# Values of the short set first, from channel-major inputs that are not normalised, in a hybrid mLSTM and dilated-attention encoder layer

## The chip, the cores and the metric

The kernel runs on one core of one Trainium2 chip. The metric is the device time of one execution in microseconds (us). Times of several executions are given as a median with the lowest and the highest.

## The reference

One encoder layer is applied with the same weights to two token sets, the long set A (1024 tokens) and the short set B (512 tokens), each token with 1024 channels, all in float32:

```
h      = x * rsqrt(mean(x*x) + eps) * pre_w            # RMSNorm over channels
cols   = h @ w_in                                      # 1024 -> 12304 columns
m_qk, m_v, m_o, m_z, m_i, m_f, a_qkv, a_z, gate = split(cols)
y_m    = mlstm(conv_silu(m_qk), m_v, m_i, m_f) * sigmoid(m_o) * silu(m_z)
y_a    = dilated_attention(a_qkv) * silu(a_z)
merged = sig(g_A) * (y_m @ w_pm) + sig(g_B) * (y_a @ w_pa)
out    = x + RMSNorm(merged @ w_out) * post_w
```

The change touches only the first two lines, and of the columns above all the "values": `m_v` (1024 columns), the attention's v (1536) and the 16 columns of the mLSTM gates, 2576 together. The row norm is one number per token. It therefore commutes with the projection: `(x * r * pre_w) @ w = r * ((x * pre_w) @ w)`.

## The kernel before, in words

**Three matmuls for one.** To keep float32 accuracy at TensorE's fast rate, each operand is split into a high part (a rounded copy, made by ScalarE) and a low part (the difference, made by VectorE), and `mm3` (L190 to L195) issues high x high, high x low and low x high into one PSUM bank. Weights are split on the fly, for the fill in `split_w` (L244).

**The long set's projection** is a 2 x 2 block product, tokens in two halves of 512 and channels in two halves of 512, done with seven products in place of eight. The seven combined inputs are `B11`, `T2`, `B21`, `T3`, `T1`, `T4`, `B22`, each four tiles of 128 channels by 512 tokens, split and kept in SBUF as `H`. The combined weights are made by `sums`. The value columns are done in four groups (`value_group`, g = 0 to 3), each group two blocks of `VW` = 322 columns. One product of a group is 48 matmuls with H as the stationary operand and 322 columns moving. The other columns are done by `unit_pair`, with 512 tokens moving.

**Group 0** differs from the other groups, because it also makes `H`. The tokens arrive row-major (tile `xt`, 128 tokens x 1024 channels). `root` (L253) squares a row tile on ScalarE with a running sum and computes the reciprocal root on GpSimd. `combos` returns four helpers: `lead` makes B11 by multiplying four row tiles by diagonal matrices of the root on TensorE, `norm` normalises row tiles, `sub` forms differences on VectorE, and `put` transposes a combined input into PSUM by 128 x 128 matmuls on TensorE, from where ScalarE and VectorE take the high and low parts. The generators `with_m1`, `with_m2`, `with_m7`, `with_m6` place these between the matmuls of group 0's products, in the order M1, M2, M7, M6, M5, M4, M3. A row of `pre_w` is spread over all partitions by four 512-wide matmuls (L1882) first.

**The short set's projection** is not blocked. It is done in units of 128 columns (`unit`, 24 matmuls of 512 tokens in eight steps) and, for the values, ten units of 256 columns (`value_unit`, the first with the 16 gate columns, `VG` = 272; per unit four token tiles of 24 matmuls, 16 steps of six matmuls). The units are not a stage of their own. They are a list in `Fill`, and the later stages (mLSTM of A, attention of A, mLSTM of B) call `fill(share)` between their own matmuls, so that TensorE always has work. `STEPS` says how many steps each stage takes from the list and `SHORT` is their total: 310 + 232 + 194 = 736. The list begins with eight attention units, then the ten value units. The short set's `H` (`hT`) is made by `short_input` behind the last unit of A: 32 transposes of row tiles (`xs`) that were loaded and normalised during the last eight pairs of units.

**Order of the work.** TensorE runs in the order in which the program is written (`manual_schedule`). In the first part of the program the other engines and the DMA queue of SyncE (SP) are ordered by the compiler by priority and readiness; from the fill on SP is written by hand too. `tc.issue_after(x)` keeps instructions of an engine behind x, and `high_priority` pulls weight splits forward. All PSUM products of the first part share eight banks (`d`).

The lines that the steps name: L249/L250 weight splits of the fill; L256 to L258 root; L273, L279, L280 `turn_in` (transposes of the short set's input and their high and low parts); L315 a 512-wide matmul of the bias tables; L347, L349 `lead`; L377, L379, L387 `put`; L426/L427 weight splits of the value groups; L1022 to L1044 `front` and L1078 to L1106 `core` of the long mLSTM (rm, scl, qw, ql, kl, cf, cl); L1463 to L1500 attention.

Of the kernel before, what the change touches and what calls it, by code (L numbers as in the profile page):

```python
# [43 lines left out]
VG = 256 + 16  # L44
RING = 4 * VG
# [131 lines left out]
class Net:  # L177
# [83 lines left out]
    def norm(self, xt, r, junk, pw=None):  # L261

        r = self.root(xt, r, junk)
        if pw is None:
            return self.nc.vector.tensor_scalar(xt, xt, r, None, op0=OP.mult)
        return self.nc.vector.scalar_tensor_tensor(xt, xt, r, pw, op0=OP.mult, op1=OP.mult)

    def turn_in(self, parts, ps, out, k, w=None):

        nc = self.nc  # L270
        p = ps.tile([P, BLK], F32, name="d")
        for t, x in enumerate(parts):
            nc.tensor.transpose(p[:, t * P:(t + 1) * P], x[:, k * P:(k + 1) * P], self.ident)  # L273
        hi, lo = (x[:, k] for x in out)
        if w is None:
            end = nc.scalar.activation(hi, p, AF.Copy)
            nc.vector.tensor_sub(lo, p, hi.bitcast(F32))
        else:
            end = nc.scalar.activation(hi, p, AF.Copy, scale=w)  # L279
            nc.vector.scalar_tensor_tensor(lo, p, w, hi.bitcast(F32), op0=OP.mult, op1=OP.subtract)  # L280
        return end


    def constants(self, pool):
        nc, a = self.nc, self.a
        self.ident = pool.tile([P, P], F32, name="ident")
        make_identity(nc, self.ident)
        self.mhalf = pool.tile([P, 1], F32, name="mhalf")
        nc.vector.memset(self.mhalf, -0.5)
        self.prew = pool.tile([P, KT], F32, name="prew")  # L290
# [39 lines left out]
    def combos(self, ps, H, xt, r, junk, pw, minus, again, diag):  # L330

        nc = self.nc
        part = lambda i, j: [x[:, j * BLK:(j + 1) * BLK] for x in xt[i]]
        a0, b0, a1, b1 = part(0, 0), part(0, 1), part(1, 0), part(1, 1)
        plus, neg = self.ident, minus.bitcast(F32)  # L340
        terms = {B21: [(b0, plus)], B22: [(b1, plus)], T3: [(b1, plus), (a1, neg)],
                 T1: [(a0, plus)], T2: [(b1, plus)], T4: [(b0, plus), (b1, neg)]}

        def lead():
            ps_ = [ps.tile([P, BLK], F32, name="d") for _ in range(4)]
            for t in range(4):
                nc.vector.tensor_scalar(diag[t], self.ident, self.root(xt[0][t], r[t], junk), None, op0=OP.mult)  # L347
                for k in range(4):
                    nc.tensor.matmul(ps_[k][:, t * P:(t + 1) * P], a0[t][:, k * P:(k + 1) * P], diag[t], start=t == 0,  # L349
                                     stop=True, skip_group_check=True)  # L350
            for k in range(4):
                hi, lo, w = H[0][B11][:, k], H[1][B11][:, k], self.prew[:, k:k + 1]
                nc.scalar.activation(hi, ps_[k], AF.Copy, scale=w)
                self.low = nc.vector.scalar_tensor_tensor(lo, ps_[k], w, hi.bitcast(F32), op0=OP.mult, op1=OP.subtract)  # L354

        def norm(i, t):
            if i:
                return self.norm(xt[i][t], r[4 * i + t], junk, pw)
            return nc.vector.scalar_tensor_tensor(xt[i][t], xt[i][t], r[t][:, 2:3], pw, op0=OP.mult, op1=OP.mult)

        def sub(m):
            for t in range(4):
                if m == T1:
# [4 lines left out]
        def put(m, k):  # L368

            if m == T4 and k == 0:  # L370
                again()
# [1745 lines left out]
```

## Time and profile before

| what | us |
|---|---|
| median of 3 executions (lowest, highest) | 2295.2 (2293.82, 2298.0) |
| the profiled execution | 2292.12 |
| its span, first to last instruction | 2290.3 |
| start to the first main matmul | 13.49 |
| value group 0 | 76.61 |
| value groups 1 to 3 | 156.25 |
| units of the long set | 726.78 |
| mLSTM of A, with fill (985 to 1320) | 335.00 |
| attention of A, with fill (to 1648) | 328.00 |
| mLSTM of B, with fill (to 1850) | 202.00 |
| attention of B (to 2120) | 270.00 |
| rest | 170.30 |

The stretches follow one another but for 11.87 us between the units and the mLSTM of A. PE is TensorE's matmuls, PEld its weight loads, DVE VectorE, ACT ScalarE, POOL GpSimd, SP the queue that issues most transfers. In a row of instruction groups the first number is the summed time, the second the mean in ns of one instruction, and behind the bar stands the engine's idle time before them and what ended it. The tile names are the program's, without buffer numbers. A matmul's listed duration is its latency through a pipeline, so that two neighbours overlap; the distance from start to start is what a matmul costs.

### The profile page before, as it was taken

To read this page: it belongs to the slowest core of one execution; us is meant where nothing else is said; L and a number is where in the kernel's file an instruction comes from. 1 tells how busy PE (TensorE), PEld (TensorE's weight loads), DVE (VectorE), ACT (ScalarE), POOL (GpSimd) and SP (SyncE) were. 2 spreads that over 40 slices of the span, in tenths; PEclk is the share of its full clock that TensorE was granted. 3 is DMA by queue.
4 is the path that set the end of the run, shared out by engine and by line. 5 is a ranking of instruction groups with operands and counts; after the bars stand their busy time and mean duration, and the time that the engine had idled before them with its cause. 6 is when DMAs were issued, how large, how long until landed. Compare 5 with 4: busy or idle time off the path is not lost. (4 is left out here: it accounts for less than half of the span.)

```text
span 2290.3 us, 36121 instructions
## 1 busy us (share of the span) xinstructions
PE 2258.5 (99%) x12628; PEld 1975.3 (86%) x12628; DVE 1465.7 (64%) x2851; ACT 1102.2 (48%) x2255; POOL 628.6 (27%) x824
## 2 busy tenths in 40 slices
PE   9999999999999999999999999999999999999998
PEld 8999888888878888879999889988888888888887
DVE  7765577688875564466777756674487744555563
ACT  6332243444443343366667656776544444544422
POOL 2000333333332232136556510001032221421311
PEclk9999999999999999999999999999999999999999
DMA  3552455543222243285674679987687878787673
GB/s 126 161 134 71 173 204 194 195 167 113 101 102 83 83 147 110 91 315 154 219 226 138 199 195 243 249 227 214 181 254 242 254 217 241 201 256 210 216 259 113
DMA packets 251903, 416.71 MB, mean 182 GB/s; under 512 B 24993, under 2 KB 150049, under 8 KB 251722
## 3 DMA queue, kind: packets, MB, share of 16 engines
q1 hardware_dynamic: 248120, 401.82, 56.9%
q10 hardware_dynamic: 3602, 12.59, 1.4%
q8 instruction: 100, 1.64, 0.3%
q14 instruction: 81, 0.66, 0.1%
HBM read 294.34 MB, written 128.37 MB: 185 GB/s over the span
## 5 line engine op out<-in xcount | busy, mean ns | idle before, releaser
L193 PE MATMUL dense<-H,wh 128*128 128x512 f32 x672 | 277.5, 413 | 2.3 <-DVE sw L714 1.9
L195 PE MATMUL dense<-H,wl 128*128 128x512 f32 x672 | 263.8, 393 | 0.0
L194 PE MATMUL dense<-H,wh 128*128 128x512 f32 x672 | 263.0, 391 | 0.0
L195 PE MATMUL d<-Hh,phla 128*128 128x512 f32 x608 | 237.0, 390 | 2.2 <-DVE phla L610 2.2
L193 PE MATMUL d<-Hh,phla 128*128 128x512 f32 x608 | 236.6, 389 | 0.0
L194 PE MATMUL d<-Hl,phla 128*128 128x512 f32 x608 | 236.6, 389 | 0.0
L250 DVE TENSOR_TENSOR wl<-wraw,wh 128x1024 fp32r<-128x1024 f32 (+1 forms) x130 | 163.9, 1262 | 106.7 <-ACT wh L249 105.4
L1475 DVE CUSTOM_DVE_ANT_0 ls<-lg,bias 128x256 f32<-128x256 f32 (+1 forms) x288 | 93.7, 361 | 158.9 <-PE lg L1463 53.9
L249 ACT ACTIVATE wh<-wraw 128x1024 fp32r<-128x1024 f32 (+1 forms) x130 | 137.0, 1054 | 97.1 <-PE dense L194 50.0
L628 POOL TENSOR_TENSOR psum_w<-pw_raw 128x512 f32<-128x512 f32 x38 | 61.4, 1617 | 443.4 <-DVE u L596 216.0
L1479 ACT ACTIVATE ls<-ls,nm 128x256 f32<-128x256 f32 (+1 forms) x288 | 130.0, 453 | 102.9 <-DVE nm L1477 87.8
L195 PE MATMUL d<-Hh,phlb 128*128 128x512 f32 x456 | 177.4, 389 | 0.0
L193 PE MATMUL d<-Hh,phlb 128*128 128x512 f32 x456 | 177.4, 389 | 0.0
L194 PE MATMUL d<-Hl,phlb 128*128 128x512 f32 x456 | 177.4, 389 | 0.0
L195 PEld LDWEIGHTS dense<-H,wl 128*128 128x128 f32 x672 | 126.2, 188 | 28.7
L193 PEld LDWEIGHTS dense<-H,wh 128*128 128x128 f32 x672 | 126.6, 188 | 20.4 <-issue 2.3
L194 PEld LDWEIGHTS dense<-H,wh 128*128 128x128 f32 x672 | 127.0, 189 | 17.5
L194 PE MATMUL d<-vlo,Hh 128*128 128x322 f32 x448 | 139.9, 312 | 1.9 <-DVE vlo L427 1.9
L193 PE MATMUL d<-vhi,Hh 128*128 128x322 f32 x448 | 141.0, 315 | 0.3
L195 PE MATMUL d<-vhi,Hl 128*128 128x322 f32 x448 | 140.3, 313 | 0.4 <-DVE Hl L354 0.2
L195 PEld LDWEIGHTS d<-Hh,phla 128*128 128x128 f32 x608 | 114.1, 188 | 27.3 <-DVE phla L610 3.7
L194 PEld LDWEIGHTS d<-Hl,phla 128*128 128x128 f32 x608 | 114.1, 188 | 23.7
(573 smaller groups left out, 6064.2 us busy)
## 6 DMA issues: line engine op xcount, KB each, us to landing
pw_raw<-w_in SPq DMA_DIRECT2D x76, 512.0 KB
wraw<-w_in SPq DMA_DIRECT2D x76, 512.0 KB
aqk_a<-pwk SPq DMA_DIRECT2D x48, 512.0 KB
aqk_b<-sw SPq DMA_DIRECT2D x48, 256.0 KB
wraw<-w_pm SPq DMA_DIRECT2D x24, 512.0 KB
wraw<-w_out SPq DMA_DIRECT2D x24, 512.0 KB
wraw<-w_v SPq DMA_DIRECT2D x18, 512.0 KB
erep<-erow SPq DMA_DIRECT2D x16, 512.0 KB
```

The source lines that it names most:

```text
L193: nc.tensor.matmul(out, lh, rh, start=start, stop=False)
L194: nc.tensor.matmul(out, lh, rl, start=False, stop=False)
L195: nc.tensor.matmul(out, ll, rh, start=False, stop=stop)
L249: self.splits = (nc.scalar.activation(hi[:, :n], raw[:, :n], AF.Copy), nc.vector.tensor_sub(lo[:, :n], raw[:, :n], hi[:, :n].bitcast(F32)))
L250: nc.vector.tensor_sub(lo[:, :n], raw[:, :n], hi[:, :n].bitcast(F32)))
L628: self.nc.gpsimd.tensor_add(s[:, 0], ws[1][:, 0], ws[1][:, 1])
L1475: nc.vector.tensor_tensor_reduce(out=ls[:, hh], in0=ts["lg"][hh], in1=bt[:, hh], scale=1.0, scalar=NEG, op0=OP.add, op1=OP.max, accum_out= ...
L1479: nc.scalar.activation(ls[:, hh], ls[:, hh], AF.Exp, bias=nm[:, hh:hh + 1], accum_out=ot[:, 128 + hh:129 + hh])
```

## The change

The short set's values are computed first of all, in a stage of their own. The inputs come also in a channel-major layout (`x_prompt_t`, `x_sample_t`: 128 channels x 512 tokens per tile, made on the host as a mere transposition like the weights' layouts), so nothing is transposed on the chip. The short set's tiles are scaled by `pre_w` and split, not normalised (`load`), into `HB`, which takes the places of T4 and B22 of `H`. `short_values` runs eight column groups of 322 with the same weights (`w_vp`) that the value groups read later; the row scale `r` is applied when a product leaves its PSUM bank. `scale(i)` loads row tiles (two buffers) for the three blocks of 512 tokens, takes `root` of each and writes diagonal matrices; `row_of` turns four of them with a matrix of ones into a tile `R[i]` that holds the row scales along the free axis on all partitions. With R, `combos` normalises the long set's channel-major tiles and forms and splits the seven combined inputs on VectorE and ScalarE, piece by piece beside column groups 3 to 7. Group 0 is then written as groups 1 to 3 were. The short set's `hT` is made from channel-major tiles normalised with `R[0]` during the last pairs of units. The ten value units leave the fill: `SHORT` becomes 576, `STEPS` (210, 202, 164, 290, 86); six more gate units stand ahead of the convolution units. Cut to its core:

```diff
-    def combos(self, ps, H, xt, r, junk, pw, minus, again, diag):
...
+    def row_of(self, ps, diag, row):
+        p = ps.tile([P, BLK], F32, name="d")
+        for t in range(4):
+            self.nc.tensor.matmul(p[:, t * P:(t + 1) * P], self.ones, diag[t], start=t == 0, stop=True, skip_group_check=True)
+        self.nc.scalar.activation(row, p, AF.Copy)
+    def norm(self, x, j, k, row):
+        w = self.prew[:, 4 * j + k:4 * j + k + 1]
+        self.nc.vector.scalar_tensor_tensor(x[:, k], x[:, k], w, row, op0=OP.mult, op1=OP.mult)
+    def parts(self, hl, k, x):
+        hi, lo = hl[0][:, k], hl[1][:, k]
+        end = self.nc.scalar.activation(hi, x[:, k], AF.Copy)
+        self.nc.vector.tensor_sub(lo, x[:, k], hi.bitcast(F32))
+    def combos(self, H, xq, R):
...
+        for k in range(4):
+            self.norm(a0, 0, k, R[0])
+            self.parts(at(B11), k, a0)
+        yield
...
+    def short_values(self, T, H, load, vw, sb, ps, r, first):
...
+        for b in range(8):
+            raw = raws[b % 2]
+            banks = [ps.tile([P, BLK], F32, name="d") for _ in range(4)]
+            for kh in range(2):
+                hi, lo = (vw.tile([P, N], F32R, name=x, bufs=2) for x in ("vhi", "vlo"))
+                with self.tc.high_priority():
+                    nc.scalar.activation(hi, raw[:, kh], AF.Copy)
+                    nc.vector.tensor_sub(lo, raw[:, kh], hi.bitcast(F32))
+                wh, wl = (z.rearrange("p (k c) -> p k c", c=VW) for z in (hi, lo))
+                if b == 0:
+                    load(kh)
+                for i in range(4):
+                    for j in range(4):
+                        t, k = (j, i) if b == 0 else (i, j)
+                        ts = slice(t * P, (t + 1) * P)
+                        self.mm3(banks[t][:, :VW], (H[kh][0][:, k, ts], H[kh][1][:, k, ts]), (wh[:, k], wl[:, k]),
+                                 kh == k == 0, kh == 1 and k == 3)
+            if b < 6:
+                raws[b % 2] = vw.tile([P, 2, N], F32, name=("va", "vb")[b % 2], bufs=1)
+                fetch(b + 2)
...
+                    nc.scalar.activation(z[:, 0, :w], x, AF.Copy, scale=s)
...
-        units = [x for u in range(4) for x in pair(u)] + [self.value_unit(u, T) for u in (0, 4, 1, 5, 2, 6, 3, 7, 8, 9)]
-        units += [az(i) for i in range(4)] + gates[:6]
+        units = [x for u in range(4) for x in pair(u)] + [az(i) for i in range(4)] + gates[:12]
...
-SHORT = 736
-STEPS = (310, 232, 194, 290, 86)
+SHORT = 576
+STEPS = (210, 202, 164, 290, 86)
...
+                def scale(i):
+                    diag[i] = []
+                    x = (B.x, A.x, A.x[BLK:])[i]
+                    for t in range(4):
+                        row, d = p0.tile([P, D], F32, name="row", bufs=2), p0.tile([P, P], F32, name="dg", bufs=4)
+                        nc.sync.dma_start(row, x[t * P:(t + 1) * P])
+                        diag[i].append(d)
+                        nc.vector.tensor_scalar(d, N.ident, N.root(row, r[4 * i + t], row), None, op0=OP.mult)
...
+                steps = N.short_values(B, HB, load, vw, p0, ps, r, first)
+                next(steps)
...
+                xq = [[xp.tile([P, 4, BLK], F32, name=f"xq{2 * i + j}") for j in range(2)] for i in range(2)]
+                for i in range(2):
+                    for j in range(2):
+                        nc.sync.dma_start(xq[i][j], a[x1 + "_t"][i, j])
+                N.row_of(ps, diag[0], R[0])
+                scale(1)
+                next(steps)
+                N.row_of(ps, diag[1], R[1])
+                scale(2)
+                next(steps)
+                N.row_of(ps, diag[2], R[2])
+                combos = N.combos(H, xq, R[1:])
+                for _ in steps:
+                    next(combos)
...
```

More of the change, by code (lines that the diff above doesn't have):

```diff
@@ L577, in value_group @@
-        if g == 0:
-            with self.tc.issue_after(low[2]):
-                s1 = split(s[:, 0])
-        else:
-            s1 = split(s[:, 0])
+        self.sums(wa, wb, s)
+        m1 = product(B11, split(wa[:, 0], first))
+        for t in range(4):
+            nc.scalar.activation(u2[t], m1[t][:, :VW], AF.Copy)
+        w12 = split(wa[:, 1])
+        s2 = split(s[:, 1])
+        nc.vector.tensor_sub(s[:, 1], wa[:, 1], s[:, 1])
+        yield
+        m2 = product(B21, w12)
+        co = co()
@@ L826, in short_units @@
             units += [z_unit(i), o_unit(i)]
-        return units + [x for u in range(4, 12) for x in pair(u)] + gates[6:]
+        return units + [x for u in range(4, 12) for x in pair(u)] + gates[12:]
     def gates_of(self, T, t):
```

408 lines of the change are left out of this document (128 added, 280 removed).

## The prediction

> **What bounds the kernel now.** The page first: which engine is never idle.
>
> ```profile
> PE 2258.5 (99%) x12628; PEld 1975.3 (86%) x12628; DVE 1465.7 (64%) x2851; ACT 1102.2 (48%) x2255; POOL 628.6 (27%) x824
> ```
>
> TensorE is busy 99% of the span, but a matmul's span is pipelined, so the share does not say how much work there is. Next, busy time by stretch. I set the borders at the first main matmul (13.49), the end of value group 0 (90.10), the end of group 3 (246.35), the end of the long set's units (973.13), and at the ends of the long mLSTM, the long attention and the short mLSTM. Columns: stretch, its length, busy time and count per engine, granted TensorE clock, DMA share, GB/s.
>
> ```profile
> 0.00:13.49 13.49, 10.00 (x37) 7.30 (x37) 4.55 (x16) 9.42 (x16) 4.82 (x19) 1.00 0.88 337
> 13.49:90.10 76.61, 74.91 (x537) 73.00 (x538) 62.04 (x86) 37.50 (x67) 7.06 (x6) 1.00 0.30 99
> 90.10:246.35 156.25, 154.38 (x1019) 151.78 (x1018) 95.84 (x171) 48.38 (x77) 6.46 (x4) 1.00 0.47 126
> 246.35:973.13 726.78, 724.59 (x3195) 598.73 (x3193) 494.87 (x518) 286.78 (x300) 232.60 (x190) 1.00 0.37 134
> ...
> 985.00:1320.00 335.00, 329.94 (x2429) 312.08 (x2428) 235.20 (x552) 218.66 (x541) 187.00 (x310) 1.00 0.65 207
> 1320.00:1648.00 328.00, 325.98 (x2096) 291.82 (x2095) 188.86 (x639) 218.57 (x646) 25.46 (x70) 1.00 0.81 218
> 1648.00:1850.00 202.00, 200.28 (x1147) 173.75 (x1146) 144.84 (x348) 92.10 (x156) 51.94 (x88) 1.00 0.78 238
> ```
>
> Every stretch is TensorE's, so the change is worth the TensorE time it removes, less the new waits. Time per matmul must be read from start to start in the timeline: a product of 48 matmuls in a value group, and one step (6 matmuls) of a short value unit in the fill.
>
> ```profile
> 136.44 0.31 PE L193 MATMUL d<-vhi,Hh 128*128 128x322 f32 x1
> ...
> 143.67 0.31 PE L193 MATMUL d<-vhi,Hh 128*128 128x322 f32 x1
> ...
> 1110.94 0.28 PE L193 MATMUL dense<-wh,H 128*128 128x256 f32 x1
> ...
> 1111.65 0.28 PE L193 MATMUL num<-ch,qh 128*128 128x258 f32 x1
> ```
>
> A product takes 7.23 us, 0.151 us a matmul of 322 columns; a step takes 0.71 us, 0.118 us a matmul of 256 (the listed 0.31 and 0.28 are latencies).
>
> **The change part by part.** *Short values.* Removed: 10 value units of 4 token tiles of 24 matmuls, 960 x 0.118 = 113.6 us; I take 116, since four tiles are 272 wide and each of the 40 starts a fresh bank. Added ahead of everything: 8 column groups x 2 halves x 48 = 768 matmuls, 16 x 7.23 = 115.7 us. The columns are the same, so this moves work and saves nothing.
>
> *Group 0.* Its 76.6 us hold seven products (50.6) and the transposes, pair matmuls and waits that build the combined inputs. Afterwards it is written like groups 1 to 3, which take 156.25 / 3 = 52.1: -24.5 us. The combined inputs become VectorE and ScalarE work beside the short products.
>
> ```profile
> L427 DVE TENSOR_TENSOR vlo<-vb,vhi 128x1288 fp32r<-128x1288 f32 x8 | 12.0, 1495 | 2.5 <-ACT vhi L426 2.5
> ...
> L383 DVE TENSOR_TENSOR Hl<-d,Hh 128x512 fp32r<-128x512 f32 x16 | 10.6, 685 | 7.7 <-ACT Hh L381 7.7
> ```
>
> VectorE there: 16 weight splits x 1.50 = 24, and 16 normalisations, 16 subtractions and 36 low parts x 0.69 = 47; with diagonals and evictions I estimate 82 us, ScalarE's splits, high parts, squares and evictions 75, both in 118 us of TensorE work. Hidden, with a third to spare. If that cover went, T4 and B22, last to be made, would be late at the sixth product of group 0. SP has some 75 transfers to issue, loads and stores in one queue, so a row load that waits for its buffer holds what stands behind it; each block leaves 14.5 us for that. GpSimd gets twelve short root chains and is otherwise idle there (6.46 us of 156.25).
>
> *Start.* The four first matmuls, the transfer rate, the first row square and the first weight split:
>
> ```profile
> 3.38 3.75 PE L1882 MATMUL d<-Hh,u 1*128 1x512 f32 x4 [3.38 <-DMA Hh<-prew]
> ...
> 194.88 1.05 PE L315 MATMUL d<-oh,tb 128*32 128x512 f32 x2
> ```
>
> ```profile
> 4.00:13.49 9.49, 9.38 (x37) 6.80 (x35) 4.04 (x9) 7.83 (x14) 3.71 (x10) 1.00 1.03 413
> ```
>
> ```profile
> 4.57 1.06 ACT L256 ACTIVATE Hl<-x 128x1024 fp32r<-128x1024 f32 x1 [1.27 <-DMA x<-x_prompt]
> ...
> 10.06 0.74 ACT L426 ACTIVATE vhi<-va 128x644 fp32r<-128x644 f32 x1 [0.37 <-DMA va<-w_vp]
> ```
>
> Before, four row tiles and half a weight block (2.76 MB) had to land by 10.06; at 413 GB/s that is 6.7 us from about 3.4. Now two channel tiles and that half block (1.18 MB) do: 3.4 + 2.9 = 6.3. The first matmul needs the split's high part (1.3 us, by 0.74 for half of it), the second its low part (1.5): 9.1, so that the stream stands as if begun at 8.9, against 13.49: -4.6 us. The four matmuls at 3.38 took 0.94 us each, two of the same length at 194.88 took 0.52: at the start TensorE ran at about half speed, though the clock row says 1.00. Before, that fell on set-up; now on the first product. Bounds: nothing, to half of the 10 us from 3.38 to 13.49, 5 us. I take 2, near the 1.7 that those four lost.
>
> *Row sums.* Three sets of four 128-wide matmuls: 1.3 us. Their wait matters more: TensorE runs in written order, and the first set stands behind block 0 and ahead of block 1, so all later products queue behind it. It needs the last of four row tiles, which share two buffers; the last two rows are issued only when the first two have been squared (some 14 us), behind what SP has sent by then. Landing then: x 2.1 MB, weights 2.6, rows 2.1, and (the other 1.1 reuse buffers still being read) 3.1 of the long set's 4.2 MB by channel, 9.9 MB: 3.4 + 24 = 27.4; the square of 1.06, with root and diagonal about as long again, makes 29.6. Block 0 ends at 8.9 + 14.5 = 23.4: a wait of 6.2 us. With no long inputs ahead it is 0; with all of them and the next block's weights (2.4 MB) it is 12. I take 6. The other two sets have 14.5 us more each for their 2.1 MB of rows: about in time. The set takes a fifth PSUM bank, so block 1's fourth tile waits for block 0's first eviction, which needs the first row tile's root alone: no later than the wait above. A wait also costs clock:
>
> ```profile
> 1889.71 0.79 PE L194 MATMUL dense<-K,wh 128*128 128x512 f32 x1 [0.84 <-POOL K L1679]
> ```
>
> ```profile
> 1891.00:1899.00 8.00, 7.59 (x28) 0.50 1.00 299
> ```
>
> After short waits like this one around 1889 the granted clock was 0.50 for 8 us, 4 us lost. I take 2 (0 to 4).
>
> *Long mLSTM, long attention, short mLSTM.* The fill falls from 736 to 576 steps: 310 to 210, 232 to 202, 194 to 164. An ordinary step is three matmuls of 512, each 726.78 / 3195 = 0.227 us by the units' stretch, 0.68 in all. The first stage loses the 160 value steps (116 us) and takes 60 ordinary ones back (41): -75, 335 to 260. The others lose 30 each, -20.5. New stalls: VectorE in the first stage keeps 235.2, less 20 splits of 1.23 and 16 low parts, plus 7.5 other units: some 216 of 260, 83%. A stretch of this very stage runs so without a gap on TensorE:
>
> ```profile
> 1251.60:1288.00 36.40, 36.40 (x212) 31.84 (x212) 30.10 (x65) 25.05 (x58) 21.13 (x32) 1.00 0.99 268
> ```
>
> So I take +4 there and +1 for each of the others, whose DMA shares of 0.81 and 0.78 rise to some 0.87 with the same bytes in less time. Bounds for the three: -3, where short waits beside the value units go, to +25.
>
> *Border after the units.* 32 transposes go. But VectorE's low parts were what the first dense unit followed, and its weight splits still stand ahead:
>
> ```profile
> 973.93 2.35 DVE L250 TENSOR_TENSOR wl<-wraw,wh 128x1024 fp32r<-128x1024 f32 x2
> 976.20 4.04 DVE L280 SCALAR_TENSOR_TENSOR H<-d,prew,H 128x512 fp32r<-128x512 f32 x6
> ```
>
> ```profile
> 978.07 0.48 PE L193 MATMUL dense<-H,wh 128*128 128x512 f32 x1
> ```
>
> The first low part comes at 976.9 with or without transposes, so not 5 us but 1.1 are won. The short rows' four norms become eight VectorE instructions inside the 726.8 us of units: nothing.
>
> **Sum.** -4.6 - 24.5 + 115.7 + 1.3 + 2 + 6 + 2 (front: +97.9) - 116 - 1.1 + 6 = -13.2 us. The profiled execution took 2292.1, 1.8 more than its span; it becomes 2278.9. It lies 3.1 below the runs' median of 2295.2, so I add that: 2282. A measurement here cannot tell 0.2% (4.6 us) from no change.
>
> **Rivals.** [...] In the long mLSTM, VectorE instructions with two SBUF inputs and GpSimd's seem to exclude each other (after each name: shortest, median, longest in ns):
>
> ```profile
> L1082 DVE TENSOR_TENSOR cl<-cf,ch x56: 675/810/1166, 1009.2 to 1315.2; 128x516 fp32r<-128x516 f32 x56
> L250 DVE TENSOR_TENSOR wl<-wraw,wh x35: 1207/1226/1564, 998.0 to 1313.9; 128x1024 fp32r<-128x1024 f32 x33, 128x1088 fp32r<-128x1088 f32 x2
> L1044 DVE SCALAR_TENSOR_TENSOR kl<-K,col,kh x56: 460/482/1014, 994.6 to 1302.0; 128x256 fp32r<-128x256 f32 x56
> L1033 POOL TENSOR_TENSOR qw<-Q,rw x56: 723/1072/1376, 989.7 to 1307.3; 128x256 f32<-128x256 f32 x56
> L1037 POOL TENSOR_TENSOR ql<-qw,qh x56: 726/742/1469, 991.3 to 1314.8; 128x256 fp32r<-128x256 f32 x56
> L1029 POOL TENSOR_TENSOR scl<-rm,sch x64: 452/466/1313, 993.6 to 1310.6; 128x128 fp32r<-128x128 f32 x64
> ```
>
> ```profile
> 1220.86 1.16 DVE L1082 TENSOR_TENSOR cl<-cf,ch 128x516 fp32r<-128x516 f32 x1
> ```
>
> The longest times are about the shortest plus a partner's. At their shortest these six come to 37.8 + 42.2 + 25.8 + 40.5 + 40.7 + 28.9 = 216 us of 335, 64%; without 12.5 splits (15) 201 of 260, 77%. If in-order queues can load such a lock to 68% only, the stage ends at 296 in place of 264: 2314. It decides below 71% (283, 2301); 64% is the most that is seen. [...]
>
> *The row scales come later still.* For it speaks the order of issue on SP, against it that 14.5 us per block stand between the sets. If the second and third row sets queue behind stores and weights too, three waits add up to 25 us with the clock's share: 15 more than taken, 2297, no change.
>
> *All is hidden.* For it speaks that SP may issue the row tiles ahead of the long set's, against it the slow first matmuls. Neither waits nor cold clock nor stalls: 16 us less, 2266.
>
> *The gain of the two later stages fails to come,* for DMA: with 25 of their 41 us lost, 2305: TensorE waits there for tiles that land late. For it speaks the DMA share; against it that TensorE had hardly a gap at that share.
>
> **How the numbers follow.** Forecast with its bounds (2270 to 2292): 0.54; all hidden (2262 to 2270): 0.12; late row scales: 0.11; port: 0.17; DMA: 0.06. Faster, below 2290.6: 0.54 + 0.12 less 0.01 at the upper edge, 0.65; same: 0.11, that 0.01 and 0.03 of the last two, 0.15; slower, above 2299.8: 0.20. The range 2262 to 2304 leaves out most of the port's case and half of DMA's; the likeliest case alone spans 2270 to 2292.
>
> **What would show it.** Group 0 near 52 us with no 128-wide matmuls between its products; first 322-wide matmul before 9 us; the gap ahead of the row-sum matmuls; the long mLSTM near 264 us; cl and qw medians, if the port binds. The prediction is wrong if that stage stays over 283, or if the waits ahead of the row sums pass 20 us.

## The result: 1.0% slower, and the profile after

The changed kernel takes 2318.39 us (median of 4; 2317.78 to 2318.62) beside 2295.61 us of the kernel before (median of 4; 2293.82 to 2298.0): 1.0098 times, 95% interval 1.0081 to 1.0116. The forecast was 2282, range 2262 to 2304. The profiled execution took 2317.78 us, its span is 2316.0, 25.7 longer than before.

The page's first part, for the changed kernel:

```profile
PE 2238.7 (97%) x12192; PEld 1953.7 (84%) x12192; DVE 1483.9 (64%) x2884; ACT 1108.1 (48%) x2248; POOL 626.4 (27%) x824
```

There are 436 matmuls fewer and TensorE is busy 20 us less, in a span that is longer: work went and waits came. Where, is seen by stretch. The borders now are the first unit, the first fill matmul behind the units, the first logits of the long attention, the first products of the short scan (the mLSTM of B) and the first logits of the short attention; first the kernel before, then the changed one (columns as in the prediction):

```profile
0.00:246.35 246.35, 239.30 (x1589) 232.08 (x1590) 162.43 (x271) 95.30 (x159) 18.34 (x29) 1.00 0.44 129
246.35:978.07 731.72, 728.44 (x3226) 602.11 (x3225) 499.62 (x524) 290.35 (x306) 233.04 (x198) 1.00 0.37 134
978.07:1328.15 350.08, 345.01 (x2499) 324.40 (x2498) 243.54 (x563) 227.71 (x555) 188.49 (x315) 1.00 0.65 208
1328.15:1651.15 323.00, 320.98 (x2071) 287.84 (x2070) 186.09 (x635) 214.33 (x638) 24.10 (x67) 1.00 0.81 219
1651.15:1851.65 200.50, 198.78 (x1140) 172.52 (x1139) 145.73 (x348) 92.16 (x155) 51.94 (x88) 1.00 0.79 241
1851.65:2290.30 438.65, 425.96 (x2113) 356.38 (x2111) 228.32 (x513) 182.34 (x442) 112.72 (x128) 0.99 0.72 217
```

```profile
0.00:350.60 350.60, 324.80 (x2145) 321.66 (x2145) 204.68 (x333) 136.96 (x223) 11.99 (x34) 0.98 0.53 161
350.60:1082.95 732.35, 728.21 (x3192) 600.99 (x3193) 499.40 (x525) 286.14 (x297) 240.28 (x184) 1.00 0.37 135
1082.95:1375.95 293.00, 279.66 (x1726) 248.74 (x1725) 230.56 (x540) 208.01 (x509) 180.31 (x322) 0.98 0.66 209
1375.95:1687.25 311.30, 302.82 (x1978) 272.69 (x1977) 181.27 (x629) 208.19 (x630) 24.61 (x68) 0.99 0.84 219
1687.25:1872.65 185.40, 177.51 (x1044) 154.23 (x1044) 139.26 (x344) 85.61 (x148) 54.35 (x88) 1.00 0.79 238
1872.65:2316.00 443.35, 425.68 (x2114) 355.40 (x2112) 228.74 (x515) 183.15 (x442) 114.87 (x128) 0.99 0.71 216
```

Busy time hides waits, as the prediction warned. So I add up, per stretch, what the matmuls cost by their width when nothing waits (start to start 0.227 us for 512 columns, 0.147 for 322, 0.119 for 256 and 258, 0.111 for 128, 0.084 for 64, 0.125 for 272), and, as gaps, every interval that is over 60 ns longer, by how much it is longer. A half clock counts as a gap. What is left to the length are intervals within those 60 ns, in the front the time ahead of the first matmul (3.4 and 8.5 us), in the rest the last 7 us. The third kernel is the best of the experiments (e14, below).

| us: length, matmul time, gaps | before | after | e14 |
|---|---|---|---|
| front (to the first unit) | 246.3, 226.2, 14.7 | 350.6, 314.2, 25.2 | 331.9, 314.2, 6.6 |
| units | 731.7, 728.1, 4.5 | 732.4, 724.6, 8.6 | 727.5, 724.6, 3.9 |
| long scan (mLSTM of A) | 350.1, 340.7, 11.2 | 293.0, 268.8, 24.4 | 292.1, 268.8, 23.4 |
| long attention | 323.0, 299.9, 19.4 | 311.3, 278.8, 28.2 | 305.3, 278.8, 22.1 |
| short scan | 200.5, 195.5, 5.3 | 185.4, 173.7, 12.2 | 177.4, 173.7, 5.3 |
| rest | 438.7, 406.6, 21.9 | 443.4, 406.6, 26.2 | 441.1, 406.6, 24.1 |
| sum | 2290.3, 2197.0, 77.0 | 2316.0, 2166.7, 124.8 | 2275.3, 2166.7, 85.4 |

The change takes 30.3 us of matmuls away. New gaps of 47.8 us eat them and, with 8.2 us outside matmul time and gaps (5.1 of them ahead of the first matmul), make the span 25.7 us longer. Three places are seen at once. First, the row sums: start, duration, and in brackets the wait and who ended it.

```profile
8.50 0.63 PE L192 MATMUL d<-vhi,Hh 128*128 128x322 f32 x1 [8.50 <-ACT vhi L370]
...
34.28 0.80 PE L312 MATMUL d<-dg,ones 128*128 128x128 f32 x2 [7.04 <-DVE dg L1748]
38.68 0.80 PE L312 MATMUL d<-dg,ones 128*128 128x128 f32 x2 [3.60 <-DVE dg L1748]
```

Second, the border to the units, which the prediction did not have at all; SP's own waits of the same time stand below it:

```profile
345.09 0.31 PE L194 MATMUL d<-vhi,Hl 128*128 128x322 f32 x1
350.60 0.80 PE L192 MATMUL d<-Hh,phla 128*128 128x512 f32 x1 [5.20 <-ACT phla L521]
```

```profile
SPq L535 <- PE d L194: 11.4, 1, 11.4
SPq L535 <- DVE vlo L433: 1.6, 1, 1.6
```

SP waits 11.4 us for TensorE before it may load the units' first raw weights: their buffer lies where the last product still reads its operands. Third, the scans and the attention: the waits of TensorE in the long scan, then the longest in the long attention, then the longest in the short scan (total us, times, longest). In these rows `hn` is a round's normalised result, which TensorE transposes some rounds later; `num` needs a PSUM bank that is free when `r` (the denominators) and `X` (the running result) have been taken from it; `st` are the scores, `lg` the attention's logits, and `H` is here the split input of the short set.

```profile
PE a L976 <- ACT hn L969: 4.8, 3, 2.2
PE dense L193 <- DVE H L322: 3.4, 1, 3.4
PE num L192 <- DVE r L958: 1.8, 1, 1.8
PE a L871 <- ACT st L864: 1.6, 1, 1.6
PE num L192 <- ACT X L961: 1.5, 2, 1.3
```

```profile
PE lg L1335 <- DVE ot L1347: 6.2, 1, 6.2
```

```profile
PE a L1175 <- ACT hn L1168: 6.6, 6, 1.3
```

In order of time, 5.0 us of the long scan's waits (H and st) stand ahead of its first round, 1.5 (X) within rounds, and 6.6 (hn and r) where one head ends and the next begins.

### The profile page after: what moved, and what is told of

The parts are those of the page before. It is cut to its first block, busy times and chain, and to the rows that moved or that the text cites. A ratio compares the mean times of both kernels' runs of the same rounds, so it can differ in the third digit from the quotient of the medians.

```text
span 2316.0 us, 35313 instructions
## 1 busy us (share of the span) xinstructions
PE 2238.7 (97%) x12192; PEld 1953.7 (84%) x12192; DVE 1483.9 (64%) x2884; ACT 1108.1 (48%) x2248; POOL 626.4 (27%) x824
## 5 line engine op out<-in xcount | busy, mean ns | idle before, releaser
L192 PE MATMUL dense<-H,wh 128*128 128x512 f32 x672 | 282.2, 420 | 0.0
L193 PE MATMUL dense<-H,wh 128*128 128x512 f32 x672 | 265.4, 395 | 3.4 <-DVE H L322 3.4
L192 PE MATMUL d<-vhi,Hh 128*128 128x322 f32 x704 | 221.9, 315 | 8.5 <-ACT vhi L370 8.5
L193 PE MATMUL d<-vlo,Hh 128*128 128x322 f32 x704 | 220.8, 314 | 1.5 <-DVE vlo L371 1.5
L194 PE MATMUL d<-vhi,Hl 128*128 128x322 f32 x704 | 220.8, 314 | 0.0
L249 DVE TENSOR_TENSOR wl<-wraw,wh 128x1024 fp32r<-128x1024 f32 x110 | 137.8, 1254 | 75.4 <-ACT wh L248 73.1
L248 ACT ACTIVATE wh<-wraw 128x1024 fp32r<-128x1024 f32 x110 | 115.8, 1053 | 66.7 <-PE dense L193 33.8
L193 PEld LDWEIGHTS dense<-H,wh 128*128 128x128 f32 x672 | 128.5, 191 | 17.3 <-DVE H L322 3.8
L192 PEld LDWEIGHTS d<-vhi,Hh 128*128 128x128 f32 x704 | 134.5, 191 | 9.5 <-ACT vhi L370 8.5
L192 PEld LDWEIGHTS d<-Hh,phla 128*128 128x128 f32 x608 | 114.9, 189 | 30.3 <-ACT phla L521 6.7
L194 PEld LDWEIGHTS d<-Hh,phla 128*128 128x128 f32 x608 | 114.8, 189 | 29.4 <-DVE phla L522 5.7
```

The lines of the kernel that those rows point to most:

```text
L192: nc.tensor.matmul(out, lh, rh, start=start, stop=False)
L193: nc.tensor.matmul(out, lh, rl, start=False, stop=False)
L194: nc.tensor.matmul(out, ll, rh, start=False, stop=stop)
L248: self.splits = (nc.scalar.activation(hi[:, :n], raw[:, :n], AF.Copy), nc.vector.tensor_sub(lo[:, :n], raw[:, :n], hi[:, :n].bitcast(F32)))
L249: nc.vector.tensor_sub(lo[:, :n], raw[:, :n], hi[:, :n].bitcast(F32)))
```

## The experiments

e1 to e4 edit the changed kernel, e5 keeps the edits of e1 and e2, and the others build on the run that the table names. Each was timed beside the kernel before on the same chip. Its median moved from 2289.9 to 2293.3 from one timing to the next, so the ratios compare better than the times. After, again, is 1.0098. Gaps and lengths come from one profiled execution of each kernel. In the seven kernels whose long scan has the same instructions and steps (after, e1, e2, e3, e5, e10, e14) its gaps are 21.7 to 26.0 us, so a difference inside that band shows nothing; in the short scan the band is narrow, 11.5 to 12.3 (after, e1 to e3, e5, e7, e8, e10, e12).

| run | us | ratio to before, 95% |
|---|---|---|
| e1 rows early | 2314.80 | 1.0094 (1.0069 to 1.0118) |
| e2 raw first | 2309.09 | 1.0070 (1.0047 to 1.0093) |
| e3 both | 2306.05 | 1.0059 (1.0039 to 1.0079) |
| e4 both, fill weighted | 2320.16 | 1.0125 (1.0099 to 1.0151) |
| e5 both, inputs later | 2293.25 | 1.0009 (0.9996 to 1.0022) |
| e6 e5, more steps in the scans | 2296.90 | 1.0016 (1.0002 to 1.0030) |
| e7 e5, no low parts on GpSimd | 2290.76 | 0.9987 (0.9977 to 0.9996) |
| e8 e5, chain first | 2294.25 | 1.0009 (0.9995 to 1.0023) |
| e9 e5, light VectorE | 2279.12 | 0.9955 (0.9941 to 0.9970) |
| e10 e5, table first | 2286.55 | 0.9982 (0.9966 to 0.9997) |
| e11 e10, steps | 2287.73 | 0.9990 (0.9979 to 1.0000) |
| e12 e10, later turn in the long scan | 2293.30 | 1.0004 (0.9994 to 1.0013) |
| e13 e10, later turn in both | 2286.67 | 0.9972 (0.9962 to 0.9982) |
| e14 e10, later turn in the short scan | 2279.23 | 0.9954 (0.9937 to 0.9971) |
| e15 e14, scores on GpSimd | 2281.41 | 0.9955 (0.9941 to 0.9970) |
| e16 e14, light VectorE, later turn in the long scan | 2271.32 | 0.9913 (0.9888 to 0.9939) |

### The front: e1, e2, e3, e5

e1 gives row tiles 2 and 3 of the short set a buffer that is still free:

```diff
-                        row, d = p0.tile([P, D], F32, name="row", bufs=2), p0.tile([P, P], F32, name="dg", bufs=4)
+                        row = more[t - 2] if i == 0 and t > 1 else p0.tile([P, D], F32, name="row", bufs=2)
```

> Of the changed kernel, only the home of the short set's row tiles 2 and 3 differs: a buffer that is still free, so that all four row loads are issued ahead of the long set's inputs. Theory (order of issue): the 11.6 us that TensorE idles ahead of the first row sums is transfer time queued behind the long set's inputs, so it falls under 2 us, block 1 starts near 28 us in place of 39.1, and the time becomes 2306 (2303 to 2309). Rival (root chain): the wait is the square, root and diagonal of four tiles on ScalarE, GpSimd and VectorE, which the transfers merely accompany; then over 6 us of it stay and the time is 2312 or more.

Neither: the first set's wait is gone, and the second set waits in its place.

```profile
42.30 0.61 PE L312 MATMUL d<-dg,ones 128*128 128x128 f32 x4
49.33 0.80 PE L312 MATMUL d<-dg,ones 128*128 128x128 f32 x2 [6.42 <-DVE dg L1752]
50.60 0.80 PE L312 MATMUL d<-dg,ones 128*128 128x128 f32 x2 [0.48 <-DVE dg L1752]
```

8.2 us of such waits in place of 10.6. The stretches of the changed kernel say why: from 14 to 34 us the DMA engines have no time left.

```profile
14.00:24.00 10.00, 10.00 (x65) 10.00 (x65) 4.05 (x5) 4.53 (x8) 1.49 (x4) 1.00 1.01 410
24.00:34.00 10.00, 3.24 (x23) 3.05 (x22) 2.63 (x4) 3.74 (x8) 0.74 (x2) 0.93 1.01 410
34.00:44.00 10.00, 6.12 (x26) 5.83 (x27) 1.58 (x4) 4.19 (x9) 0.93 (x3) 0.56 0.96 355
```

A DMA share of 1.01 and 410 GB/s until 34, and 0.96 with 355 GB/s up to 44: in e1 the rows that were moved forward came in time, and TensorE waited 6.42 us for those of the second set. e2 changes only the order in which the unit stage's buffers are laid out:

```diff
+        for u in (ua, ub):
+            w = sb.tile([P, 2, BLK], F32, name="pw_raw", bufs=4)
...
         us = [sb.tile([P, BLK], F32, name=f"pu{i}", bufs=4 - i) for i in (2, 3)]
         bs = [sb.tile([P, 2, 2, BLK], F32R, name="phlb", bufs=2) for _ in range(2)]
```

> Of the changed kernel, only the order in which the unit stage's buffers are laid out differs: the raw weights come first, so that they lie on a weight buffer of the value groups that is done early and not on the low parts that the last product still reads. Theory (address): the 5.4 us gap ahead of the first unit goes, and with it the half-speed matmuls behind it (5.0 us): 2308 (2305 to 2311). Rival (order on the queue): the raw weights stand in SP's queue behind the group's stores and land late wherever they lie; then the gap stays over 3 us and the time over 2313.

The raw weights are issued at 331.79 in place of 345.43, and the wait of 5.2 is 1.0 us:

```profile
PE d L192 <- ACT phla L521: 1.0, 1, 1.0
PE d L194 <- DVE phla L522: 0.5, 1, 0.5
```

The front is 345.7 long in place of 350.6 and the units 726.6 in place of 732.4: 10.7 us, of which 4.2 are the wait itself, some 3 the clock granted in the 6.10 us behind it (0.50), and the others shorter waits of later pairs of units, which e2 had fewer of. The address was the cause. How it came about is read from the program and not tried in a run: the change moved the sums' buffer (`vsum`) to the other side of SBUF, the buffers behind it moved up, and the raw weights came to lie on the low parts of the last product.

> Both edits together, nothing else. If the two places are independent the gains add: 2318.4 - 12 - 10 = 2296 (2292 to 2300), the time before the change. The stages after the units then still carry some 33 us of new gaps. If what is won early only moves a wait to a later stage, the time stays over 2302.

The front fell to 343.2, 7.4 below after (e1 alone 3.6, e2 alone 4.9). The time of 2306.05 misses the forecast of 2296, as e1 had not brought what it should. e5 keeps both and issues the long set's inputs behind the rows of the set that needs them; it also puts the long set's second row sums one block later:

```diff
+                    with tc.issue_after(diag["at"].ins):
+                        for j in range(2):
+                            nc.sync.dma_start(xq[i][j], a[x1 + "_t"][i, j])
```

> Both edits of the run before (early row tiles, raw weights first), and now the long set's inputs by channel, 4.2 MB, are issued behind the row tiles of the set that needs them, and the long set's second row sums stand one block later. Theory (bandwidth): the row sums wait because in the first 44 us the transfers run at their limit (DMA share 1.0, about 410 GB/s), so that moving one set forward only makes the next set late; asking for 6 MB less by then leaves under 2 us of waits at the row sums in place of 8.4: about 8 us less than with the two edits alone, 2298 (2295 to 2302). Rival: the long set's rows are late because each needs one of two buffers; then 5 us or more stay at the second set.

No wait at the row sums is left, and the front is 332.1 long. In the same slices TensorE is full while the DMA share is still 0.93 and 0.99:

```profile
24.00:34.00 10.00, 10.00 (x72) 10.00 (x71) 4.29 (x8) 6.36 (x16) 2.23 (x6) 1.00 0.93 308
34.00:44.00 10.00, 10.00 (x70) 10.00 (x69) 3.73 (x5) 4.66 (x6) 0.74 (x2) 1.00 0.99 404
```

The later place is not what did it: in e5 the second set's last diagonal is written at 41.00, ahead of the block's end at 41.56, where the set stood before; in e3 it was written at 50.26, behind 41.94. So bandwidth, and the order of what is asked for, was the cause; from e2 to e5 the front lost 13.6 us, the full price of those waits with their clock (0.56 from 34 to 44 us in the changed kernel, 1.00 in e5). The ratio fell from e3's 1.0059 to 1.0009, some 11 us where 8 had been forecast. With the front mended the kernel takes as long as before the change: the 30 us of matmuls are still eaten, by the later stages.

### The later stages: e4, e6 to e8

e4 deals the same number of fill steps out otherwise:

```diff
-                fill(1 / 3)
-                core(k)
+                share = (1.6 if i in (0, n - 1) else 0.8) / 3
+                fill(share)
+                core(k, share)
```

> Both edits, and the same number of fill steps per stage dealt out otherwise: in the long mLSTM a head's first and last rounds (8 and 7 of the scan's ends, which are short) take 1.6 shares, the others 0.8; in the short mLSTM a third of a share moves from behind the hn transposes to ahead of them. Theory (latency): the new gaps there are the chain from a head's last product to its hn transposes, which the thinner fill no longer covers (about 14 us with the clock that they cost in the long, 8 in the short); half to three quarters of that goes: 2283 (2278 to 2289). [...]

It got worse, beyond the 2293 to 2297 us set down for the case that VectorE and GpSimd together are the limit: the long scan's gaps rose from 21.7 (e3) to 34.7 us, since now the ordinary rounds, with 0.8 shares, waited: all 7.1 us of the waits for X lie in them, and half of the 6.9 for hn, the other half still at the change of head. In the short scan, where a third of a share went ahead of the transposes, they rose from 12.2 to 14.2, which no theory had. TensorE's waits in the long scan of e4:

```profile
PE a L976 <- ACT hn L969: 6.9, 7, 2.4
PE num L192 <- ACT X L961: 5.3, 5, 1.6
...
PE num L192 <- DVE X L964: 1.8, 2, 1.3
```

e6 changes `STEPS` to (236, 166, 174), e7 sets two low parts to zero on GpSimd (`memset` for `tensor_sub`; if GpSimd's subtractions hold VectorE up, cl should run near 0.68 us, the gaps fall under 10 us and the time to 2286), e8 wraps the denominators and the normalisation in `high_priority`.

> The same, with fill steps dealt out 236, 166 and 174 to the long mLSTM, the long attention and the short mLSTM in place of 210, 202 and 164. Theory (the two scans lack cover, the attention does not): the long mLSTM grows by 17.7 us of matmuls and loses 6 to 10 of its some 22 us of gaps, the short one grows by 6.8 and loses 3 to 5 of 12, the attention shrinks by 24.5 and gains at most 3: 8 us less than without it, 2290 (2286 to 2294). Rival (transfers): the attention, with a DMA share of 0.84 already, cannot run shorter; it keeps 10 us or more of the 24.5, and the time is 2298 or more.

> As the run with the inputs later, but in the long mLSTM GpSimd sets the low parts of scores and of weighted queries to zero in place of subtracting: GpSimd's 64 + 56 subtractions with two SBUF inputs are left out (that part of the result with them), all other work stays. [...] In-order chain: the waits are for the root and the normalisation behind other work on VectorE and ScalarE, which stay; gaps 17 or more, 2293 to 2298.

> As the run with the inputs later, but in the long mLSTM the denominators, the sums and the normalisation of a round are given priority on VectorE, ScalarE and GpSimd over the weight splits and the next round's preparation. In-order chain: the waits for X and hn (8 us of matmul waits with the clock that they cost as much again) halve: 2292 (2288 to 2296). [...]

e6: 26 steps more left the long scan's gaps at 24.1 us (e5: 26.0), and ten more raised those of the short one from 12.3 to 16.5; the attention gave its 28.2 us without a new gap, at a DMA share of 0.87. So the rival by transfers is out, and the theory that more fill covers the scans too (2296.90 us for a forecast of 2290). e7: GpSimd's subtractions lengthen an instruction of VectorE, and that is not what binds. Of VectorE's cl, first e5, then e7 (after the count: shortest, median, longest in ns):

```profile
L954 DVE TENSOR_TENSOR cl<-cf,ch x56: 678/810/1240, 1090.1 to 1344.0; 128x516 fp32r<-128x516 f32 x56
```

```profile
L954 DVE TENSOR_TENSOR cl<-cf,ch x56: 669/696/1243, 1089.3 to 1340.4; 128x516 fp32r<-128x516 f32 x56
```

The median falls from 810 to 696 ns, near the forecast of 0.68 us, and the long scan's gaps only from 26.0 to 23.1, inside the band of the unedited. The 56 products `qw` on GpSimd, 43.1 us, have two SBUF inputs too and stay; a run without them was not made. e8: gaps 25.5, the same waits; priority alone does nothing.

### Which wait ends last: e9 to e16

e9 gives only the first 64 of 1024 columns of each fill unit's weights a low part:

```diff
-                       nc.vector.tensor_sub(lo[:, :n], raw[:, :n], hi[:, :n].bitcast(F32)))
+                       nc.vector.tensor_sub(lo[:, :m], raw[:, :m], hi[:, :m].bitcast(F32)))
```

> As the run with the inputs later, but of each fill unit's weights only the first 64 of 1024 columns get their low part on VectorE (until the short set's fill ends); the other low parts stay at zero, so that part of the fill's result is left out. It takes some 33 us of VectorE's 257 us of instructions out of the long mLSTM. Theory (load): two rounds of waits after two edits that changed nothing, the stage's gaps come from VectorE being full: they fall from 26 us to 14 or less, those of the short mLSTM from 12 to 7 or less: 2275 to 2284. Rival (latency): the waits are the length of a round's chain from product to transposes over three engines, whoever is full; gaps stay over 20 and the time within 5 us of 2293.

VectorE is busy 202.8 us in the long scan in place of 229.3, and it is a half: the short scan's gaps fall from 12.3 to 4.7, as under load; the long one's from 26.0 to 20.0, or 1.7 below the least of the unedited. There the waits of num for r and X go (3.3 us to 0.2), that for H falls from 3.4 to 1.4, and those for hn stay. TensorE's waits in the long scan of e9:

```profile
PE a L977 <- ACT hn L970: 5.6, 3, 2.2
...
PE dense L193 <- DVE H L323: 1.4, 1, 1.4
```

e10 holds the fill's stores back while the long scan ends, so that they stand behind the attention's first bias table:

```diff
-                self.tick()
+                self.tick(lambda p: p[1][0] == "ym")
```

> As the run with the inputs later, but the stores of fill results that are still pending at the end of the long mLSTM are issued behind the attention's first bias table and not ahead of it. Theory (head of the queue): the 6.2 us wait at the third logits, and some 2 to 3 us of clock behind it, came from SP waiting 5 us for a convolution's result before it could issue the table; of these 8 to 9 us half or more goes: 2288 (2285 to 2291). Rival: the table is late for its own transfer or for the hn stores that stay ahead of it; then the wait stays over 5 us and the time at 2293.

In the changed kernel SP's queue ran like this. It waits 5.1 us for a convolution's result ahead of the store to `qk_b`, and the table (`bias`) is issued behind that. The third logits need a bank that is free only when the first softmax, with the table, has read it:

```profile
1374.44 0.36 SPq L208 DMA_DIRECT2D ym_a<-ym  x1
1379.97 0.33 SPq L208 DMA_DIRECT2D qk_b<-sw  x1
1380.35 0.43 SPq L208 DMA_DIRECT2D ym_a<-ym  x1
1380.87 0.94 SPq L229 DMA_DIRECT2D bias<-erep  x2
```

In e10 the wait for the logits is 1.6 us in place of e5's 6.0, and the attention 305.0 long in place of 311.8. The theory holds. The row in e10:

```profile
PE lg L1335 <- DVE ot L1347: 1.6, 1, 1.6
```

e11 adds `STEPS` (244, 168, 164):

> As the run with the table first, with fill steps 244, 168 and 164 in place of 210, 202 and 164: only from the attention to the long mLSTM. In the run with 236, 166 and 174 a step given to the long mLSTM cost 0.59 us there, and one taken from the attention saved 0.79: 34 steps make 34 x 0.2 = 7 us: 2281 (2277 to 2286). If the attention is at the limit of its transfers (share 0.87 in that run), it saves less than 0.68 a step and the time stays at 2288.

A miss: the 34 steps cost the long scan 23.1 us and saved the attention 24.4, one for one. What e6 seemed to gain by them was not in the steps. e12 moves the long scan's hn transposes one round back, e13 does it for the short scan too, e14 for the short scan alone:

```diff
-                turns.pop(k - 3, lambda: None)()
+                turns.pop(k - 4, lambda: None)()
...
-                turns.pop(k - 1, lambda: None)()
                 fill(2 / 3)
                 core(k, 1)
+                turns.pop(k - 1, lambda: None)()
```

> As the run with the table first, but in the long mLSTM the hn transposes of a round stand four rounds behind it and not three. Theory (latency at the head changes): taking a seventh of VectorE's work out of the stage removed the waits for X but not those for hn, 5 to 6 us at the three head changes, where the rounds are short; one round more covers them: hn waits under 1.5 us, and with the clock that they cost 5 to 8 us less: 2280 (2277 to 2283), faster than before the change by 0.3 to 0.5%. Rival (the same wait under another name): the chain's engines are late as a whole, the next instruction of TensorE in line waits in hn's place (num for X, kv for the sums), and the time stays within 2 us of the run with the table first.

> As the run before, and in the short mLSTM a round's hn transposes stand behind the next round's second core and not ahead of it. Theory (latency): the 7 us of hn waits there go too, gaps of that stage from 12 to 6: 2275 (2272 to 2279). Theory (load, from the run with light weights on VectorE, where these gaps fell to 4.7): the wait moves to the next product, the stage's gaps stay over 10 us and the time within 2 us of the run before.

> The run with the table first, with the later hn transposes in the short mLSTM alone; the long one keeps its three rounds. If what the two runs before showed holds (latency in the short scan, load in the long one), the short scan's gaps are 5 to 6 us in place of 12 and the others stay: 6 us less than the run with the table first, 2280 (2277 to 2284), 0.4 to 0.6% faster than before the change. If the long scan's lag did not matter, it is 2286, like the run before.

In the long scan the rival won: no wait for hn is left, and the next in line waits instead, 11.0 us (gaps 28.2, e10: 23.7). TensorE's longest waits in the long scan of e12:

```profile
PE num L192 <- ACT X L961: 6.6, 3, 3.1
PE num L192 <- DVE r L959: 3.6, 1, 3.6
```

In the short scan the consumer's later place is enough: its gaps fall from 11.9 to 5.4 (e13) and 5.3 (e14), before the change 5.3, and no wait for hn is left. The longest wait in the short scan of e14:

```profile
PE num L194 <- POOL scl L1141: 1.1, 1, 1.1
```

A lighter VectorE (e9) was enough there too, so the late result and the early reader are two sides of one wait. e13's time misses its 2275 by the long scan, whose gaps are 30.3 with the later turn. e14 takes 2279.23 us, 0.46% less than before the change, within its forecast, and leaves nothing out; it beats both, and no later version that leaves nothing out is faster. e15 moves the product of mask and scores to GpSimd (`nc.gpsimd.tensor_tensor(rm, rm, st[h % 2][:, c], op=OP.mult)`), e16 adds the edits of e9 and e12 to e14:

> The same, and in the long mLSTM the product of a round's mask with its scores (128x128, 64 times, 27 us of VectorE) is made on GpSimd, which there has 181 us of work in some 293, as against VectorE's 256. Load on VectorE: its share falls by a tenth, the waits for X (5 us and their clock) go, gaps of that stage from 24 to 18: 2275 (2272 to 2279). [...]

> The run with the later turn in the short mLSTM, and in the long one both remedies that failed or half failed alone: low parts of only 64 of 1024 columns of the fill's weights on VectorE (the others stay zero, so that part of the fill's result is left out) and hn transposes four rounds behind. Theory (two limits, the second behind the first): relieving VectorE takes the waits for X, the later turn takes those for hn, so that the long scan's gaps fall from 23 us to 12 or less, the level before the change, and its length from 292 to 281 or less. Rival (a third engine, ScalarE or the clock of the round itself): gaps stay at 18 or more.

e15: gaps 24.1, the waits for X 0.9 us in place of 2.1 and those for hn 5.9 in place of 4.2; no gain at 2281.41 us. The wait for scl, which GpSimd makes from that product, is only 0.8 us. e16: gaps 19.6, so its rival; of the 8 us that its profiled execution lies below e14's, 4.6 are in the long scan (287.5 for 292.1) and as much in the rest, which the edits do not touch (436.5 for 441.1). What holds the long scan stays open: about 20 us of gaps, no one wait over 2.6 us in sum in e16, and each remedy for one of them turns it into another.

## Why the prediction was wrong, step by step

| step of the sum, us | forecast | measured | from |
|---|---|---|---|
| start, group 0, short products, row sums, slow first matmuls | +89.9 | +85.8 | 350.6 - 246.3, less the two waits in the front (13.6 and 4.9) |
| waits ahead of the row sums, with clock | +8 (0 to 16) | +13.6 | front of e2 against e5 |
| wait of the first unit, with clock | none | +10.7 | after against e2 |
| border, units | -1.1 | -5.1 | 732.4 - 731.7, less the 5.8 by which e2 shortens the units |
| fill | -116 | -114.8 | matmul time of the three stages |
| new stalls in the three stages | +6 (-3 to 25) | +31.0 | their length less matmul time |
| rest | 0 | +4.7 | 443.4 - 438.7 |
| sum | -13.2 | +25.9 | span +25.7 |

Right were the moved work (the terms of start and fill within some 4 us; group 0 took 49.9 us, from 143.20 to 193.10, with no transpose between its products), the first main matmul before 9 us (8.50), the slow first matmuls (0.27 us from start to start from 10.47 to 15.30, 0.15 behind it, some 2 us lost), and the place and kind of the wait at the row sums. Right was the border too: the long scan's first wait, 3.4 us for H, is the low part that the border term had priced, and the table counts it with the stalls. Counted with the border it leaves -1.7 there for the forecast -1.1, and +27.6 for the stalls. The wait at the row sums cost 13.6 in place of 8, since I had the last row's diagonal at 29.6 and the matmul that needs it ran at 38.68: the long inputs went ahead of the rows as forecast, and all transfers together ran at 410 GB/s up to 34 us, longer than my 9.9 MB.

The step that failed most is the stalls term, +6 in place of +31 (27.6 without the wait for H), beyond its bound of 25 either way. I argued it from VectorE's share (83% forecast; 230.56 of 293.00, 79%, measured, so the load was not underrated) and from one stretch of 36 us in which TensorE had no gap at that load. That stretch lay inside the rounds. The new waits are for the most part at the places that it did not contain: the entry of the long scan, head changes, where rounds are short, and the border to the attention, where a convolution unit now stood that used to lie later. Shown of the 31: 6.8 by the table behind a store (e10), 7.6 by the short scan's consumer (e10 to e14). The long scan's growth of 13.2 in gaps (9.8 without the wait for H) is not cured by any run; a relieved VectorE leaves 20.0 (e9) and 19.6 (e16) where the unedited have 21.7 to 26.0. Its cause stays open.

The step that was missing is the first unit's wait. I followed every instruction that was moved, and no buffer: `vsum` changed sides, and I did not ask whose memory the next stage's first load would then be given.

Of the rivals, the one in which VectorE and GpSimd hold each other up (`port` in the chances) came closest in time, but its own sign stayed out: the long scan with its fill shrank by 57.1 us, so its old stretch of 335 became 278, under the 283 at which that rival was to decide, and taking GpSimd's subtractions away (e7) won no more than some 3 us. No run shows a port: what is shown is the median of cl, 810 ns with GpSimd's subtractions and 696 without. Counted like the 278, the stage was forecast near 264 and took 278. The row scales' rival had the mechanism of e1 (the next set waits too), but in the changed kernel only the first set waits, at a price of 13.6 and not 25. The DMA rival is out: the attention shrank by another 24.4 us when asked to (e11), at a DMA share of 0.89. Neither of my two conditions for being wrong was met (278 under 283, 13.6 under 20); no condition watched the border to the units, the attention or the short scan. The stalls' miss of 25 us alone puts the forecast of 2282 at 2307, past the end of the range at 2304; the first unit's wait (10.7) and the row sums (5.6) add to it. The rest's +4.7 is not shown to be the change's: the same instructions took 436.5 to 449.6 us there in the changed kernel and its edits. The range had no case in which several small waits appear at once.

## What to carry to other kernels

Price the cover that is taken away at the borders of a stage and at its shortest rounds, by what waits there already, not by its best stretch. When a buffer moves, look up whose memory the next stage's first load gets, and who still reads there. Where the DMA engines have no time left (a share of 1.01 here) order the loads by when they are due: in e1 those moved forward left 8.2 us of waits in place of 10.6, in e5 the order left none.

## What the runs showed of the hardware

After the idle 5.2 us ahead of the units the granted clock of the changed kernel stood at 0.50 for 6.10 us, 13 matmuls of 512 columns; behind a wait of 1.84 us in the long scan (to 1172.21) it was at 0.50 for 3.41 us; around one of 1.04 us in the short scan (to 1710.53) it stayed at 1.00:

```profile
350.60:356.70 6.10, 6.06 (x13) 4.35 (x14) 2.50 (x3) 2.20 (x3) 5.69 (x4) 0.50 0.77 252
...
1172.57:1175.98 3.41, 3.41 (x14) 3.13 (x14) 0.77 (x4) 1.97 (x7) 2.73 (x11) 0.50 0.87 203
```

```profile
1709.00:1713.00 4.00, 2.96 (x15) 2.14 (x14) 1.65 (x7) 2.93 (x5) 3.00 (x4) 1.00 0.95 284
```

Waits of one length did not have one price. The wait of 2.2 us for hn at the change from the second head to the third is the same in the changed kernel (to 1242.2) and in e1 (to 1241.5). Behind it the clock stayed at 1.00 in the first and fell to 0.50 in the second; first the changed kernel, then e1:

```profile
1242.09:1245.50 3.41, 3.29 (x20) 2.89 (x20) 2.31 (x7) 2.01 (x8) 3.08 (x8) 1.00 0.66 179
```

```profile
1241.27:1244.68 3.41, 3.17 (x10) 2.79 (x11) 1.38 (x6) 1.69 (x7) 3.08 (x8) 0.50 0.62 176
```

In the changed kernel's long scan the clock was at 0.50 from 1087.23, 1172.57 and 1312.51 on, 3.41 us each, at waits of 3.43, 1.84 and 2.15 us; at the wait of 2.17 us to 1242.2 it was not. No run shows what decides it. It may be a part of the spread of gaps (21.7 to 26.0 us) between executions of the same instructions.
